# Layer 1's chunk recurrence with its small products grouped by array shape in a round, its value products one round ahead in a bank of their own, and part of its outputs on the other half of the partitions

## The chip, the cores and the metric

The kernel runs on one core of a Trainium2 chip, as one program with one launch. The metric is the device time in microseconds (us). The kernel before takes 2222.28 us (median of 3 runs, 2222.04 to 2224.26).

## The reference, cut to what matters

A trunk of two layers is run on a prompt of 1024 tokens (16 learned tokens ahead of it) and on a sample batch of 8 x 8 tokens. Layer 0 is a gated delta net, layer 1 an RWKV-7 mixer with 16 heads of 64. The change lies in the recurrence of layer 1:

```python
def step(S, inp):                       # one token; S is 64 x 64 for each head
    r_t, k_t, v_t, d_t, kk_t, b_t = inp
    S = (S * d_t[:, :, None, :]
         + jnp.einsum('bhvk,bhk->bhv', S, -kk_t)[..., None] * b_t[:, :, None, :]
         + v_t[..., None] * k_t[:, :, None, :])
    return S, jnp.einsum('bhvk,bhk->bhv', S, r_t)
S, y = lax.scan(step, S0, ...)
y = (y - mean) * lax.rsqrt(var + GN_EPS) * lnx_w + lnx_b      # group norm of each head
y = y + jnp.sum(r_h * k_h * r_k, -1, keepdims=True) * v_h     # bonus term
y = y.reshape(B, T, D) * jax.nn.silu(z)
return y @ w_o, ...                                           # dense output projection
```

## The kernel before

Layer 0 fills the program to about 1110 us; projections and the inverses of layer 1's chunk systems follow. The last part, from about 1800 to 2221 us, is the **wave**: layer 1's recurrence, with its output projection and part of the sample batch's state work laid between.

The tokens are cut in 3 segments of 6 chunks of 64 tokens, and the 16 heads in 8 pairs. One pair of one segment is an **item** `P`, 24 in all. The wave runs 52 **rounds**, `tau` 0 to 51; item n does its chunk steps `ci` 0 to 5 in rounds 2n to 2n+5. So three items are under way in each of 44 rounds (4 to 47), two in four rounds and one in four. Each engine runs its instructions in the order in which the code writes them. The order is written by hand: `put(tau, phase, f, prio)` books a piece of side work, `emit(tau, phase)` writes what is booked, and `fill` writes jobs of the output projection. A tile of that projection (`zo` or `do`) takes 12 matmuls with 384 columns, in two halves of 6, one in phase 2 and one in phase 3; DVE then adds it to the residual (`x<-x,zo`, line 2025).

A round does for each item, with 64 x 64 products that TensorE runs for the two heads `h` of the pair on two parts of its array:

- `step_solve`: state `rS` times `AR`, both for the system's right-hand side (`x` = 0) and for the output (`x` = 1), in the array shape 64 rows by 64 columns ("64*64" in the profile);
- `step_scores`: `UV` times `G`, the value part of the right-hand side ("128*64"), then ACT scales it into `X`;
- phase 1: side work, here the products `fG<-AR,BK` of a later item ("64*128"), every half item in one round, which DVE masks into `G` (line 1773);
- `step_inner`: `X` times the inverse `rTT` (128*64), then ACT copies the result into the U half of `UV` (line 115); `step_old` makes the decayed old state `pre`;
- phase 2: a dense half, and transposes of keys or values (`fBT`, `fVT`, 128*128);
- `step_state`: `UV` times `BT` for the new state and `UV` times `G` for the output (128*64); DVE writes `rS` (line 1906), ACT copies `y` (line 1907);
- phase 3: the other dense half, the bonus product `fbonus` with its DVE read `rbv` (line 1756), and at an item's end the transpose of `y` (`fyT`, 64*64) with its DVE read `t` (line 1937).

[...] In the wave, every item has one of the 3 banks `r` (tiles `rA`) for all its products of a round; 2 banks `f` take turns for `fG`, `fbonus`, `fBT`, `fVT` and `fyT`; one bank `z` and two banks `d` take the projection's tiles, and in the rounds up to 22 and from 30 to 38 the jobs for a segment's first four pairs use the one bank `z` alone. A reader of a bank and a writer of the same bank are kept apart by semaphores, whichever columns they touch.

A matmul on 32-bit floats is two instructions in the profile, so 4 products of an item are 8 instructions; the dense matmuls are one instruction each.

## Time and profile before

| | |
|---|---|
| median of 3 runs | 2222.28 us |
| profiled execution, its span | 2227.4 us, 5.1 us above the median (no other time of that execution is given) |
| the wave's share of the span | some 420 us, 52 rounds |
| PE busy over the span | 2142.1 us, 96% |
| DVE, ACT, POOL busy over the span | 1411.3, 1265.0, 1237.8 us |
| PE's share of the chain that ended last | 68% |
| DMA over the span | 129 GB/s from and to HBM |

The page counts an engine as busy while an instruction of it is under way, so a busy PE can still be a PE that waits for its own pipeline when the array's shape changes. A row of the timeline joins instructions of one kind that follow on each other: its start, the time until the last has ended, the group, and the number of instructions. The distance from one row's start to the next row's is what a group takes from the round. The ends of matmuls are modelled, and overlap the next group.

### The profile page before, as it was taken

The page shows a single profiled execution, that of the slowest core. Times are in us where ns is not written, and L with a number is a line of the kernel's source. Part 1 is how long each engine was busy: PE and PEld are TensorE (multiplying, and loading weights), DVE is VectorE, ACT ScalarE, POOL GpSimd, SP SyncE. Part 2 cuts the span into 40 slices and gives each one's busy share as a digit, 9 for nine tenths or more (in the row PEclk, how much of TensorE's full clock was granted, in tenths as well). Part 3 has the DMA queues.
Part 4 walks back from the last instruction along what each step waited for, and adds up shares of the span by engine and source line. Part 5 has one row for each costly group of instructions (what it writes and reads, how often), then busy time and mean ns, then how long its engine had stood idle before and what let it go on. Part 6 is the DMA issues. An engine that isn't in the chain of part 4 may idle for free.

```text
span 2227.4 us, 55333 instructions
## 1 busy us (share of the span) xinstructions
PE 2142.1 (96%) x20382; PEld 1977.4 (89%) x20382; DVE 1411.3 (63%) x3638; ACT 1265.0 (57%) x3651; POOL 1237.8 (56%) x1890
## 2 busy tenths in 40 slices
PE   8989999999999999989999999999999999999997
PEld 7879989899999989978999999998988977888886
DVE  7858575766757585975435762667546347667764
ACT  6526565556655565645433464756546466667663
POOL 3418678585858585525241442227768646666663
PEclk9999999999999999999999999999999999999997
DMA  4324242424243333435254235587885566656532
GB/s 120 84 59 133 66 123 73 114 80 115 79 115 96 101 107 76 132 78 171 91 151 105 69 102 172 180 256 199 229 242 147 160 187 166 171 150 177 160 115 88
DMA packets 495400, 291.61 MB, mean 131 GB/s; under 512 B 222345, under 2 KB 480506, under 8 KB 495130
## 3 DMA queue, kind: packets, MB, share of 16 engines
q1 hardware_dynamic: 495130, 288.08, 46.1%
q8 instruction: 161, 2.64, 0.5%
q14 instruction: 109, 0.89, 0.1%
HBM read 195.66 MB, written 92.30 MB: 129 GB/s over the span
## 4 chain that ended last, share of the span: by engine, by line
PE 68%; DVE 13%; POOL 6%; DMA 5%; ACT 4%; issue 3%; SPq 1%; DVEq 0%; POOLq 0%; ACTq 0%
PE d L129 14%; PE dz L129 7%; PE dv L129 7%; PE rA L133 6%; PE rA L129 5%; PE zo L129 3%; PE do L129 3%; PE dk L129 3%; DVE cvy L634 2%; POOL invT L692 2%; PE fG L129 2%; POOL invtmp L690 2%; PE dq L129 2%; DMA wraw<-in_gdn_w_out 1%; DVE invT L692 1%
## 5 line engine op out<-in xcount | busy, mean ns | idle before, releaser
L143 POOL TENSOR_TENSOR wlo<-wraw,whi 128x512 fp32r<-128x512 f32 x190 | 251.4, 1324 | 229.5 <-ACT whi L139 207.2
L692 POOL TENSOR_TENSOR invT<-invT,invtmp 72x31 f32<-72x31 f32 (+36 forms) x341 | 213.4, 626 | 26.7
L634 DVE SCALAR_TENSOR_TENSOR cvy<-raw,cw,cvy 128x408 f32<-128x408 f32 (+2 forms) x288 | 203.4, 706 | 29.7 <-ACT cvy L115 25.7
L690 POOL TENSOR_TENSOR invtmp<-invA,invT 72x31 f32<-72x31 f32 (+36 forms) x341 | 202.6, 594 | 20.4 <-POOL invT L678 0.8
L129 PE MATMUL d<-xc,whi 128*128 128x384 f32 (+1 forms) x640 | 180.8, 344 | 1.0 <-ACT whi L139 0.8
L139 ACT CAST whi<-wraw 128x512 fp32r<-128x512 f32 x238 | 145.7, 614 | 27.6 <-DMA wraw<-in_rwkv_w_rkvz 13.9
L129 PE MATMUL dv<-xc,whi 128*128 128x384 f32 (+1 forms) x480 | 154.5, 343 | 0.0
L129 PE MATMUL dz<-xc,whi 128*128 128x384 f32 (+1 forms) x480 | 153.0, 342 | 0.0
L115 ACT ACTIVATE w<-rA,nbp 128x128 f32<-128x128 f32 x144 | 45.2, 364 | 152.3 <-PE rA L129 149.9
L129 PEld LDWEIGHTS d<-xc,whi 128*128 128x128 f32 x640 | 118.6, 192 | 3.5 <-ACT whi L139 1.1
L129 PE MATMUL d<-xc,wlo 128*128 128x384 f32 (+1 forms) x320 | 105.5, 339 | 1.9 <-DVE wlo L143 1.9
L160 POOL TENSOR_TENSOR ors<-ovar,cvals 128x6 f32<-128x6 f32 x24 | 34.1, 1422 | 124.6 <-DVE ovar L1122 124.6
L129 PE MATMUL dz<-xa,whi 128*128 128x384 f32 (+1 forms) x288 | 102.6, 356 | 0.5 <-DVE zg L906 0.5
L129 PE MATMUL dv<-xa,whi 128*128 128x384 f32 (+1 forms) x288 | 102.5, 356 | 0.0
L129 PE MATMUL d<-xa,whi 128*128 128x384 f32 (+1 forms) x336 | 100.1, 341 | 1.3 <-ACT whi L139 0.8
L1930 POOL TENSOR_SCALAR y<-y,mv,grs 128x64 f32<-128x64 f32 x132 | 81.7, 640 | 33.1 <-DVE grs L164 27.8
L129 PEld LDWEIGHTS dv<-xc,whi 128*128 128x128 f32 x480 | 89.3, 188 | 3.5 <-issue 3.0
L959 POOL TENSOR_SCALAR Sb<-Sb,eglb 128x128 f32<-128x128 f32 x128 | 88.8, 706 | 5.9 <-DVE usc L752 2.2
L129 PEld LDWEIGHTS dz<-xc,whi 128*128 128x128 f32 x480 | 90.4, 191 | 0.7 <-issue 0.2
L129 PE MATMUL d<-xh,whi 128*128 128x384 f32 (+1 forms) x256 | 82.3, 334 | 0.0
L129 PE MATMUL d<-xl,whi 128*128 128x384 f32 (+1 forms) x256 | 82.3, 335 | 0.0
L129 PE MATMUL d<-xh,wlo 128*128 128x384 f32 (+1 forms) x256 | 82.1, 334 | 0.0
(544 smaller groups left out, 7232.1 us busy)
## 6 DMA issues: line engine op xcount, KB each, us to landing
wraw<-in_gdn_w_in SPq DMA_DIRECT2D x96, 256.0 KB
wraw<-in_rwkv_w_rkvz SPq DMA_DIRECT2D x74, 256.0 KB
Sb<-in_state_gdn SPq DMA_DIRECT2D x64, 256.0 KB
wraw<-in_rwkv_w_o SPq DMA_DIRECT2D x48, 256.0 KB
E<-drow SPq DMA_DIRECT2D x24, 384.0 KB
attn<-drow SPq DMA_DIRECT2D x24, 384.0 KB
wraw<-in_gdn_w_out SPq DMA_DIRECT2D x36, 256.0 KB
out_s_gdn<-Sb SPq DMA_DIRECT2D x32, 256.0 KB
```

Source lines behind the costliest of these rows:

```text
L115: return self.nc.scalar.activation(out, in_, func, bias=bias, scale=scale, **kw)
L129: self.nc.tensor.matmul(out, lhsT, rhs, start=start, stop=stop)
L133: self.nc.tensor.matmul(out, lhsT, rhs, start=start, stop=True, skip_group_check=True)
L139: nc.scalar.copy(hi, x)
L143: e.tensor_tensor(lo, x, hi.bitcast(F32), op=ALU.subtract)
L160: self.nc.gpsimd.tensor_tensor(y, x, half.broadcast_to(sh), op=ALU.pow)
L634: nc.vector.scalar_tensor_tensor(ys[s][:, 0:wd(s)], raws[s][:, k:k + wd(s)], cw[k], ys[s][:, 0:wd(s)], op0=ALU.mult, op1=ALU.add)
L690: v.tensor_tensor(tmp, A[:, j, j + 1:32].unsqueeze(2).broadcast_to([nb, n, m]), Tv[:, j, 0:m].unsqueeze(1).broadcast_to([nb, n, m]), op=AL ...
L692: v.tensor_tensor(Tv[:, j + 1:32, 0:m], Tv[:, j + 1:32, 0:m], tmp, op=ALU.subtract)
L959: nc.gpsimd.tensor_scalar(Sb[g][:, u], Sb[g][:, u], self.eglb[:, hv, 4 * g + u:4 * g + u + 1], None, op0=ALU.mult)
L1930: nc.gpsimd.tensor_scalar(y[:, q], y[:, q], mv[:, q, 0:1], P.rs[:, q:q + 1], op0=ALU.subtract, op1=ALU.mult)
```

## The change

The change touches only the wave.

- `step_scores` is gone. Its products become `step_values`, which runs for the items of the next round, right after `step_inner`, and writes to a bank `x` of its own (tiles `xX`). `step_solve` adds the state's part there, and `X` is read from it.
- With one bank for `x`, there are 2 banks `r` for three items: items 0 and 2 of a round share one (`P.bank = u % 2`), on different columns.
- The output part of `step_solve` (`x` = 1) goes to the other half of the array's columns and of the partitions (`hs[h ^ x]`). The products `fG` are cut in two and have the shape 64*64.
- `step_state` follows `step_values` directly; the dense half, the transposes and `step_old` that stood between inner and state come behind it.
- `fyT` writes the other half of the partitions and moves to phase 0 of round T+8, just ahead of `step_solve`; the add behind it moves to phase 1.
- The projection's jobs start half a round later, so that a tile's second half now stands in phase 2 and the next tile's first half in phase 3 of the same round. Two pieces of sample work move by a phase, and the urgent marks on `X` and `rS` go.

Counted in the order of the instructions, the changes of array shape on PE in the wave go from 421 to 169 (by the shape changed to: small shapes from 243 to 112, fG's 64*128 from 46 to 0, dense 128*128 with 384 columns from 95 to 48, transposes from 37 to 9).

The first place is PE between inner and state in a round of three items. `X`, `rTT` and `UV` are what is named above; the numbers are tiles. Before:

```order
L133 MATMUL rA_27066<-X_27067,rTT_4030_23640 64x64
L129 MATMUL do_27133<-yh_26107,whi_26840 128x384
L129 MATMUL do_27133<-yl_26108,whi_26840 128x384
L129 MATMUL do_27133<-yh_26107,wlo_26841 128x384
L129 MATMUL do_27133<-yh_26412,whi_26840 128x384
L129 MATMUL do_27133<-yl_26413,whi_26840 128x384
L129 MATMUL do_27133<-yh_26412,wlo_26841 128x384
L126 MATMUL fBT_27141<-ident_63,BK_26707 128x128 [waits DVE_49]
L126 MATMUL fBT_27141<-ident_63,BK_26707 128x128 x2
L133 MATMUL rA_27054<-UV_4025_23635,BT_26266 64x64 [waits Activation_49]
L133 MATMUL rA_27054<-UV_4025_23635,BT_26266 64x64
L133 MATMUL rA_27054<-UV_4025_23635,G_26075 64x64 x2
```

After:

```order
L133 MATMUL rA_27214<-X_27226,rTT_4030_23640 64x64 [waits Activation_49]
L133 MATMUL rA_27214<-X_27226,rTT_4030_23640 64x64
L133 MATMUL xX_27277<-UV_4026_23636,G_26502 64x64 [waits PE_49]
L133 MATMUL xX_27277<-UV_4026_23636,G_26502 64x64
L133 MATMUL xX_27277<-UV_4027_23637,G_26803 64x64 x2
L133 MATMUL xX_27277<-UV_4024_23634,G_27102 64x64 x2
L133 MATMUL rA_27214<-UV_4025_23635,BT_26401 64x64 [waits Activation_49]
L133 MATMUL rA_27214<-UV_4025_23635,BT_26401 64x64
L133 MATMUL rA_27214<-UV_4025_23635,G_26185 64x64 x2
L133 MATMUL rA_27215<-UV_4026_23636,BT_26713 64x64 x2
L133 MATMUL rA_27215<-UV_4026_23636,G_26502 64x64 x2
L133 MATMUL rA_27214<-UV_4027_23637,BT_27013 64x64 [waits Activation_49]
```

Six dense matmuls and three transposes stood between inner and state, and the waits are for each item's own copy. Now six value products stand there, and items 0 and 2 write the same tile: item 2's inner product waits for ACT's UV copy of item 0, item 0's state product for the UV copy of item 2, and item 2's state product for ACT's copy of item 0's `y`.

The second place is ACT in the same stretch. Before:

```order
L115 ACTIVATE UV_4025_23635<-rA_27054 64x128 [waits PE_49]
L115 ACTIVATE UV_4026_23636<-rA_27060 64x128 [waits PE_49]
L115 ACTIVATE UV_4027_23637<-rA_27066 64x128 [waits PE_49]
L115 ACTIVATE pre_27118<-rS_3947_23048,DC_25917 128x64 [waits Activation_49]
L115 ACTIVATE pre_27120<-rS_3948_23049,DC_26220 128x64 [waits Activation_49]
L115 ACTIVATE pre_27122<-rS_3949_23050,DC_26520 128x64 [waits Activation_49]
L139 CAST whi_27127<-wraw_26844 128x512 [waits DMAHW7_49]
L1782 COPY BT_27140<-fBT_27141 128x384 [waits PE_49]
L1907 COPY y_26356<-rA_27054 128x64 [waits DVE_49]
```

After:

```order
L115 ACTIVATE UV_4025_23635<-rA_27214 64x128 [waits PE_49]
L115 ACTIVATE UV_4026_23636<-rA_27215 64x128 [waits PE_49]
L115 ACTIVATE UV_4027_23637<-rA_27214 64x128 [waits PE_49]
L1923 COPY y_26485<-rA_27214 128x64 [waits DVE_49]
L1923 COPY y_26786<-rA_27215 128x64 [waits DVE_49]
L1923 COPY y_27085<-rA_27214 128x64 [waits DVE_49]
L1783 COPY BT_27312<-fBT_27313 128x384 [waits PE_49]
L115 ACTIVATE pre_27318<-rS_3948_23049,DC_26343 128x64 [waits Activation_49]
```

The three `pre` and the work that stood between the UV copies and the `y` copies moved behind the `y` copies; a `y` copy still waits for DVE, which updates `rS` from the same bank first.

The third place is PE at the seam of two rounds, in a round that ends an item's `y`. Before:

```order
L129 MATMUL fyT_27172<-ident_63,y_26051 64x64 x12
L126 MATMUL fBT_27188<-ident_63,BK_26707 128x128 x3
L133 MATMUL rA_27207<-rS_3948_23049,AR_26069 64x64 x4
L133 MATMUL rA_27213<-rS_3949_23050,AR_26374 64x64 x4
L133 MATMUL rA_27220<-rS_3950_23051,AR_26663 64x64 x4
L133 MATMUL rA_27207<-UV_4026_23636,G_26380 64x64 x2
L133 MATMUL rA_27213<-UV_4027_23637,G_26669 64x64 x2
L133 MATMUL rA_27220<-UV_4024_23634,G_26956 64x64 x2
L129 MATMUL fG_27244<-AR_26950,BK_26994 128x128
L129 MATMUL fG_27245<-AR_26950,BK_26994 128x128
```

After:

```order
L126 MATMUL fBT_27338<-ident_63,BK_26867 128x128 x3
L129 MATMUL fyT_27357<-ident_63,y_26168 64x64 x12
L133 MATMUL xX_27277<-rS_3948_23049,AR_26179 64x64 x2
L133 MATMUL rA_27372<-rS_3948_23049,AR_26179 64x64 x2
L133 MATMUL xX_27277<-rS_3949_23050,AR_26496 64x64 x2
L133 MATMUL rA_27373<-rS_3949_23050,AR_26496 64x64 x2
L133 MATMUL xX_27277<-rS_3950_23051,AR_26797 64x64 x2
L133 MATMUL rA_27372<-rS_3950_23051,AR_26797 64x64 x2
L129 MATMUL fG_27402<-AR_27096,BK_27166 64x128
L129 MATMUL fG_27403<-AR_27096,BK_27166 64x128
```

The transposes of `y` stay ahead of solve with the key transposes now in front of them; solve alternates between two tiles `xX` and `rA`, the value products between solve and `fG` are gone, and each `fG` product is half as wide in its weights. A bank `f` that `fyT` wrote is what the second `fG` tile takes over.

The diff, cut to its core:

```diff
             gp = [self.ps("f", 2, "G") for h in (0, 1)]
             for u in range(3):
-                for h in (0, 1):
-                    q = slice(64 * h, 64 * h + 64)
-                    self.mm(gp[h][:, 128 * u:128 * u + 128], flat(BK[q, c + u]), flat(AR[q, c + u]))
+                for x in (0, 1):
+                    for h in (0, 1):
+                        q, o = self.HS[h], self.HS[x]
+                        self.mm(gp[h][o, 128 * u:128 * u + 128], BK[q, c + u, x], flat(AR[q, c + u]))
             for h in (0, 1):
...
-            put(T - 1, 2, go, 5)
+            put(T - 1, 1, go, 5)
...
-            put(T + 2, 2, go2, 4)
+            put(T + 2, 1.5, go2, 4)
...
-            at = [(T + 6, 0, 2), (T + 6, 3, 4), (T + 7, 3, 2), (T + 8, 2, 0)]
+            at = [(T + 6, 0, 2), (T + 6, 2, 1.8), (T + 8, 0, 3), (T + 8, 1, 2.2), (T + 8, 2, 0)]
...
-    def step_solve(self, P, ci):
-        nc, t, ap = self.nc, self.t, self.ap
-        c = 6 * P.s + ci
-        if ci == 0:
-            P.y = t(ap, [128, 6, 64], "y", 5)
-        AR, S = P.AR, self.S[P.p]
-        pA = P.pA = self.ps("r", 3, "A")
-        X = P.X = t(ap, [128, 64], "X", 4)
-        hs = [slice(0, 64), slice(64, 128)]
-        if c != 1:
+    HS = (slice(0, 64), slice(64, 128))
+    def step_values(self, items):
+        p = self.ps("x", 1, "X") if items else None
+        for u, (P, ci) in enumerate(items):
+            P.pX = p[:, 64 * u:64 * u + 64]
+            for h in (0, 1):
+                self.mmx(P.pX[self.HS[h]], P.G[:, ci, h, 0:64], P.UV[:, ci, h, :], u == 0)
+    def first(self, P, part):
+        k = P.bank, part.start
+        new = k not in self.begun
+        self.begun.add(k)
+        return new
+    def step_solve(self, items):
+        t, ap, hs = self.t, self.ap, self.HS
+        self.begun = set()
+        banks = [self.ps("r", 2, "A") for _ in items[0:2]]
+        for u, (P, ci) in enumerate(items):
+            if ci == 0:
+                P.y = t(ap, [128, 6, 64], "y", 5)
+            P.bank, b = u % 2, 256 * (u // 2)
+            v = banks[u % 2]
+            P.pU, P.pY, P.pS = v[:, b:b + 128], v[:, b + 128:b + 192], v[:, b + 192:b + 256]
+            P.X = t(ap, [128, 64], "X", 4)
+            c = 6 * P.s + ci
+            S = self.S[P.p]
             for x in (0, 1):
                 for h in (0, 1):
-                    q = hs[h]
-                    a, b = (AR[q, ci, x], S[q]) if c else (P.q0[q, x].rearrange("p b r -> p (b r)"), self.ident[q, q])
-                    self.mmx(pA[q, 256 * x:256 * x + 64], a, b, x == 0)
-    def step_scores(self, P, ci):
-        nc, t, ap = self.nc, self.t, self.ap
-        c = 6 * P.s + ci
-        pA, X, G, UV, S = P.pA, P.X, P.G, P.UV, self.S[P.p]
-        hs = [slice(0, 64), slice(64, 128)]
-        for h in (0, 1):
-            self.mmx(pA[hs[h], 0:64], G[:, ci, h, 0:64], UV[:, ci, h, :], c == 1)
-        rk = self.rk2[:, 6 * P.n + ci:6 * P.n + ci + 1]
-        with self.tc.high_priority():
-            self.act(X, pA[:, 0:64], AF.Identity, scale=rk)
+                    if c == 1:
+                        continue
+                    q, o = hs[h], hs[h ^ x]
+                    l, r = (P.AR[q, ci, x], S[q]) if c else (P.q0[q, x].rearrange("p b r -> p (b r)"), self.ident[q, q])
+                    if x:
+                        self.mmx(P.pY[o], l, r, self.first(P, o))
+                    else:
+                        self.mmx(P.pX[o], l, r)
+        for P, ci in items:
+            rk = self.rk2[:, 6 * P.n + ci:6 * P.n + ci + 1]
+            self.act(P.X, P.pX, AF.Identity, scale=rk)
     def step_inner(self, items):
         for h, (P, ci) in [(h, x) for g in (items[0:2], items[2:]) for h in (0, 1) for x in g]:
-            self.mmx(P.pA[P.us, 128 + 64 * h:192 + 64 * h], P.TT[:, h, ci], P.X)
+            self.mmx(P.pU[P.us, 64 * h:64 * h + 64], P.TT[:, h, ci], P.X, self.first(P, P.us))
             if h:
-                self.act(P.UV[P.us, ci].rearrange("p h k -> p (h k)"), P.pA[P.us, 128:256], AF.Identity, scale=-1.0)
+                self.act(P.UV[P.us, ci].rearrange("p h k -> p (h k)"), P.pU[P.us], AF.Identity, scale=-1.0)
...
     def step_state(self, P, ci):
-        nc = self.nc
+        nc, hs = self.nc, self.HS
         c = 6 * P.s + ci
-        pA, G, BT, UV, S, DC = P.pA, P.G, P.BT, P.UV, self.S[P.p], P.DC
-        hs = [slice(0, 64), slice(64, 128)]
+        G, BT, UV, S, DC = P.G, P.BT, P.UV, self.S[P.p], P.DC
         if c > 0:
             for h in (0, 1):
-                self.mmx(pA[hs[h], 384:448], BT[:, ci, hs[h]], UV[:, ci, h, :])
+                self.mmx(P.pS[hs[h]], BT[:, ci, hs[h]], UV[:, ci, h, :], self.first(P, hs[h]))
         for h in (0, 1):
-            self.mmx(pA[hs[h], 256:320], G[:, ci, h, 64:128], UV[:, ci, h, :])
-        if c > 0:
-            with self.tc.high_priority():
-                if c == 1:
-                    nc.vector.tensor_scalar(S, pA[:, 384:448], DC[:, ci:ci + 1], None, op0=ALU.mult)
-                else:
-                    nc.vector.scalar_tensor_tensor(S, pA[:, 384:448], DC[:, ci:ci + 1], P.pre, op0=ALU.mult, op1=ALU.add)
-        nc.scalar.copy(P.y[:, ci], pA[:, 256:320])
+            self.mmx(P.pY[hs[1 - h]], G[:, ci, h, 64:128], UV[:, ci, h, :], self.first(P, hs[1 - h]))
+        if c == 1:
+            nc.vector.tensor_scalar(S, P.pS, DC[:, ci:ci + 1], None, op0=ALU.mult)
+        elif c > 0:
+            nc.vector.scalar_tensor_tensor(S, P.pS, DC[:, ci:ci + 1], P.pre, op0=ALU.mult, op1=ALU.add)
+        nc.scalar.copy(P.y[:, ci], P.pY)
...
             for h in (0, 64):
-                self.mm(yp[h:h + 64, 64 * q:64 * q + 64], y[h:h + 64, a + q], self.ident[h:h + 64, h:h + 64])
+                o = 64 - h
+                self.mm(yp[o:o + 64, 64 * q:64 * q + 64], y[h:h + 64, a + q], self.ident[h:h + 64, h:h + 64])
         t1 = t(self.fp, [128, 384], "t1", 1)
         nc.vector.scalar_tensor_tensor(t1[:, 0:n], yp[:, 0:n], self.lnw[:, p:p + 1], P.bv[:, x:x + n], op0=ALU.mult, op1=ALU.add)
+        yield
...
-            tag = [("d", 2), ("r", 3), ("d", 2)][q] if s == 2 else ("d", 2)
+            tag = [("d", 2), ("r", 2), ("d", 2)][q] if s == 2 else ("d", 2)
...
-        jobs += [(lambda s=s, a=a: out(s, a, a + 4, *((Z, DD) if a else (Z,))), 16, 14 + 16 * s + 2 * a, 22 + 16 * s + 2 * a) for s in (0, 1) for a in (0, 4)]
+        jobs += [(lambda s=s, a=a: out(s, a, a + 4, *((Z, DD) if a else (Z,))), 16, 14.5 + 16 * s + 2 * a, 22.5 + 16 * s + 2 * a) for s in (0, 1) for a in (0, 4)]
...
+        at = lambda tau: [(P[n], tau - 2 * n) for n in range(max(0, (tau - 4) // 2), min(24, tau // 2 + 1)) if 0 <= tau - 2 * n < 6]
         emit(-4, 3)
         for tau in range(-2, 52):
-            items = [(P[n], tau - 2 * n) for n in range(max(0, (tau - 4) // 2), min(24, tau // 2 + 1)) if 0 <= tau - 2 * n < 6]
-            each = lambda f: [f(*x) for x in items]
+            items, following = (at(u) for u in (tau, tau + 1))
             if tau < 0:
                 fill(tau + 0.3)
             emit(tau, 0)
-            each(self.step_solve)
-            each(self.step_scores)
+            self.step_solve(items)
             emit(tau, 1)
             self.step_inner(items)
-            each(self.step_old)
+            self.step_values(following)
+            for x in items:
+                self.step_state(*x)
+            emit(tau, 1.5)
             put(tau, 2, lambda: fill(tau + 0.5), 2.5)
             emit(tau, 2)
-            each(self.step_state)
+            for P_, ci in following:
+                self.step_old(P_, ci)
             put(tau, 3, lambda: fill(tau + 1), 1)
...
```

8 lines of the change are left out of this document (5 added, 3 removed).

## The prediction

> **What bounds the kernel now.** I read the page's totals first, then the wave by windows, then the order of PE's groups in two rounds with the ACT and DVE rows beside them.
>
> ```profile
> span 2227.4 us, 55333 instructions
> PE 2142.1 (96%) x20382; PEld 1977.4 (89%) x20382; DVE 1411.3 (63%) x3638; ACT 1265.0 (57%) x3651; POOL 1237.8 (56%) x1890
> 1919.60:2166.40 246.80, 246.09 (x3736) 213.99 (x3734) 171.16 (x579) 168.72 (x571) 159.04 (x197) 1.00 0.54 153
> ```
>
> The last row is a stretch of the wave: its bounds, its length, then busy time and count of PE, PEld, DVE, ACT and POOL, the granted clock, the DMA share and GB/s. PE is busy for 246.09 of 246.80 us at full clock; the others have a third free. The wave is bound by PE, so what counts is how long each group takes PE from its start to the next start. One round, on PE:
>
> ```profile
> 1964.86 0.91 PE L133 MATMUL rA<-rS,AR 64*64 64x64 f32 x24
> 1965.70 0.57 PE L133 MATMUL rA<-UV,G 128*64 128x64 f32 x12
> 1966.20 0.94 PE L129 MATMUL fG<-AR,BK 64*128 64x128 f32 x12
> 1967.07 0.68 PE L133 MATMUL rA<-X,rTT 128*64 128x64 f32 x12
> 1967.67 0.44 PE L129 MATMUL zo<-yh,whi 128*128 128x384 f32 x1
> ...
> 1968.65 0.34 PE L129 MATMUL zo<-yh,wlo 128*128 128x384 f32 x1
> 1968.83 0.49 PE L126 MATMUL fVT<-ident,fldv 128*128 128x128 f32 x3
> 1969.25 0.34 PE L133 MATMUL rA<-UV,BT 128*64 128x64 f32 x4
> ...
> 1969.65 0.29 PE L133 MATMUL rA<-UV,G 128*64 128x64 f32 x4
> 1969.77 0.29 PE L133 MATMUL rA<-UV,BT 128*64 128x64 f32 x4
> 1969.88 0.29 PE L133 MATMUL rA<-UV,G 128*64 128x64 f32 x4
> ...
> 1971.08 0.34 PE L129 MATMUL zo<-yh,wlo 128*128 128x384 f32 x1
> 1971.26 0.34 PE L129 MATMUL fbonus<-prh,bones 128*128 128x384 f32 x1
> 1971.43 0.34 PE L129 MATMUL fbonus<-prl,bones 128*128 128x384 f32 x1
> 1971.70 0.92 PE L133 MATMUL rA<-rS,AR 64*64 64x64 f32 x24
> ```
>
> In a steady stretch (1969.65, 1969.77, 1969.88) four small instructions take 0.117 us, on two parts of the array at once: 0.0585 for one instruction on its part. BT and G alternate there with no gap, so tiles and operands may change freely; the array's shape may not. Solve's 24 instructions should take 0.70 and take 0.84; scores' 12 should take 0.35 and take 0.50. Six dense ones take 1.16 (1967.67 to 1968.83), not 6 x 0.173 = 1.04 (spacing of the `fbonus` rows), and leaving that shape costs 0.27 - 0.173 = 0.10 (1971.43 to 1971.70). A change of shape thus costs about 0.145 towards a small one. To dense it is 0.10 to drain and 0.11 to load, 0.205. `fG` takes 0.87 for six pairs at about 0.11 (twice the columns), so 0.20. Transposes, between the two, I put at 0.152.
>
> **Change: what it saves.**
>
> Shape changes. Before: 243 x 0.145 + 46 x 0.20 + 95 x 0.205 + 37 x 0.152 = 69.5 us. After: 112 x 0.145 + 48 x 0.205 + 9 x 0.152 = 27.4. Saved on PE's path: **42.1**.
>
> Solve on four parts. It uses rows by h, columns by h and x, so all four 64x64 parts work at once, where two did. That four run together is seen once before, in layer 0:
>
> ```profile
> 105.31 0.64 PE L129 MATMUL usr<-Sb,kqm 128*32 128x128 f32 x16
> 105.89 0.45 PE L129 MATMUL dv<-xc,whi 128*128 128x384 f32 x1
> ```
>
> Sixteen instructions of 128 columns, each on a quarter of the columns, take 0.58, which is four times 0.11 and one change; two at a time they would take 0.88. For solve: 1088 instructions x 0.0585 x (1/2 - 1/4) = **15.9**, 0.35 in a round of three. `fG` has twice the instructions on twice the parts: nothing. The value products are the same number, only earlier: nothing. At the bounds, these two terms are 0 (parts that share rows don't overlap) and 15.9.
>
> **Change: what it makes wait.** `fVT`, `fBT` and a dense half, 1.58 us by the rows above (1967.67 to 1969.25), lay between inner and state and hid ACT's UV copies. Now 0.35 of value products lie there, and three items have two banks. The prices:
>
> ```profile
> L115 ACT ACTIVATE UV<-rA x144: 255/272/276, 1801.9 to 2195.6; 64x128 f32<-64x128 f32 x144
> L1907 ACT COPY y<-rA x144: 204/213/243, 1804.9 to 2201.1; 128x64 f32<-128x64 f32 x144
> L1906 DVE SCALAR_TENSOR_TENSOR rS<-rA,DC,pre x128: 268/284/288, 1815.7 to 2200.8; 128x64 f32<-128x64 f32 x128
> L133 PE MATMUL rA<-X,rTT x576: 222/222/367, 1801.4 to 2195.0; 128*64 128x64 f32 x192
> ```
>
> The middle figure is the median in ns. A round in which nothing dense stands between inner and state occurs once before, near the end, and shows the chain bare:
>
> ```profile
> 2145.49 0.85 PE L133 MATMUL rA<-X,rTT 128*64 128x64 f32 x12 [0.18 <-ACT X L115]
> 2146.07 0.86 ACT L115 ACTIVATE UV<-rA 64x128 f32<-64x128 f32 x3 [0.23 <-PE rA L133]
> 2146.40 0.34 PE L133 MATMUL rA<-UV,BT 128*64 128x64 f32 x4
> ```
>
> From inner's start 0.91 us go by until the first state product. By the medians, with 0.05 for a hop between engines (2146.07 + 0.27 + 0.05 = 2146.39, against 2146.40 seen), a round of three items then runs like this, counted from inner's start:
>
> - Item 0's last inner product starts at 0.17, ends at 0.39; UV0 runs 0.44 to 0.71. Item 2's inner product, in the same bank, starts at 0.76, not 0.23: **0.53**.
> - It issues for 0.23, ends at 1.16; UV2 runs 1.20 to 1.47. The value products end issuing at 1.34, so item 0's state product waits until 1.53: **0.19**.
> - Item 0's state ends 0.40 after its start; DVE begins `rS` 0.12 later (in the rows below 1976.25 + 0.29 to 1976.66) and takes 0.28, the `y` copy 0.25 with its hop. Items 0 and 1 issue 0.47. Item 2's state waits **0.64**.
>
> Three restarts, each with a weight load that nothing covers, add 0.13 (an estimate: about a third of the 0.145 that a shape change costs). Together 1.49 us in each of 44 rounds: **65.4**. Queued behind PE's waits is the whole round, since PE runs in order; ACT's next work, `pre` and the key copy, has slack. The bounds are 0 (if all of it were covered) and 75 (if each hop took 0.10).
>
> The banks `f` and `z` are next. Rows of one seam:
>
> ```profile
> 1971.46 0.55 DVE L2025 TENSOR_TENSOR x<-x,zo 128x384 f32<-128x384 f32 x1 [0.89 <-PE zo L129]
> 1971.93 0.55 DVE L1756 TENSOR_TENSOR rbv<-fldv,fbonus 128x384 f32<-128x384 f32 x1
> 1974.02 1.02 DVE L1773 TENSOR_TENSOR G<-fG,gm 128x384 f32<-128x384 f32 x2 [1.06 <-PE fG L129]
> 1976.25 0.29 PE L133 MATMUL rA<-UV,G 128*64 128x64 f32 x4
> 1976.66 0.74 DVE L1906 SCALAR_TENSOR_TENSOR rS<-rA,DC,pre 128x64 f32<-128x64 f32 x3
> 1978.17 0.92 PE L129 MATMUL fyT<-ident,y 64*64 64x64 f32 x24
> 1979.22 0.61 DVE L1937 SCALAR_TENSOR_TENSOR t<-fyT,lnw,rbv 128x384 f32<-128x384 f32 x1
> 1979.49 0.27 PE L133 MATMUL rA<-rS,AR 64*64 64x64 f32 x2
> ```
>
> - `fG`'s second tile needs the bank that `fbonus` left. From the last `fbonus` (1971.43) to the end of `rbv` 1.05 pass, 1.10 with the hop. Before, solve and scores covered it (1.61 to `fG`). Now the drain (0.27) and the halved solve (0.50 with its change) end after 0.78: 0.32 in 23 odd rounds, **7.3**.
> - In even rounds `fyT` stands just ahead of solve, and `fG` takes its bank. From `fyT`'s start to the end of `t` are 1.66, 1.71 with the hop; fyT's 24 instructions and solve issue for 0.84 + 0.35 = 1.19: 0.52 in 19 rounds, **9.9**. `t` then holds DVE; with the two `G` masks (1.02 at 1974.02) and group-norm work behind it, `rS` comes about 0.35 late there, **6.6** (an estimate: a third of the 1.02, since most of it passes while PE waits and issues).
> - In the 16 rounds whose projection uses bank `z` alone, the next tile's first half follows the last one's second half with three transposes between: 0.17 and the 0.33 that `fVT`'s 0.42 takes without the drain behind it, 0.50. The residual add begins 0.38 after the last product's start (1971.08 to 1971.46) and takes 0.55: 0.98 with the hop, so 0.48 x 16 = **7.7**. Before, the other way round, solve to inner lay between.
>
> One of these waits occurs before, a few times, and shows that PE does stand still for it:
>
> ```profile
> 1832.28 0.93 PE L129 MATMUL fG<-AR,BK 64*128 64x128 f32 x10 [0.27 <-DVE rbv L1756]
> ```
>
> **The rest.** The moved phases of sample work issue the same DMAs on SP's queue a phase earlier or later; their data are needed rounds later, and neither queue waits: 0, at most 1 us either way. The urgent marks only ordered instructions, and the order is what I used. The `finish` tag with two banks instead of three serves one tile in the last 6 us: 0 to 0.5. Waits of before that go (some 3 us in rounds like that at 2145) balance those new in the eight rounds of one or two items.
>
> **Sum.** -42.1 - 15.9 + 65.4 + 7.3 + 9.9 + 6.6 + 7.7 = +38.9 us on the profiled 2227.4, so 2266 for a profiled span; on the median 2222.3 it is **2261 us**. As a round pair: solve to the solve after next takes 14.63 us before (1964.86 to 1979.49); 58.0/22 = 2.64 less and 96.9/22 = 4.40 more make 16.4. The likeliest case's own range is 2245 to 2278, from a chain of 1.1 to 1.9 us for a round.
>
> **Rivals.**
>
> *Faster: the chain is covered.* Savings less the other waits are 58.0 - 31.5 = 26.5, so it turns at 26.5 / 44 = 0.60 us of bank waits a round. It would take one of item 2's three waits alone (0.64 at the state) with the others hidden, say by ACT and DVE starting on products well before the modelled ends of the rows. Gone entirely it gives 2196; at a third of my price (0.3 us a round) 2209. Against: at 2145.49 the first state product came 0.91 after inner's start though item 0's X was there. For: the ends are modelled, and a part of the 0.91 is the wait for the later items' X.
>
> *Slower still: the clock.* Where PE idled, the trace shows the clock fall:
>
> ```profile
> 1909.78 1.64 PE L129 MATMUL fG<-AR,BK 64*128 64x128 f32 x10 [1.75 <-DVE rbv L1756]
> 1905.00:1910.00 5.00, 3.25 (x40) 2.67 (x42) 2.06 (x6) 2.09 (x8) 1.61 (x2) 0.96 0.83 240
> 1910.00:1913.00 3.00, 3.00 (x24) 2.66 (x25) 2.87 (x9) 0.88 (x4) 2.70 (x4) 0.50 0.01 3
> ```
>
> After 1.75 us of idle PE the next 3 us ran at 0.50. An even round of mine idles for some 2.4 of 8.8 us in pieces of under 0.7. If those pieces add up, a stretch of 3.4 us at half speed costs 1.7 us in 22 rounds, +37: 2298. Against: no piece is nearly 1.75 long.
> [...]
>
> *Four parts don't overlap.* Solve's saving goes (hidden in `fG`'s wait in most rounds), and `fG` takes 0.67 longer in 46 rounds, +31: 2292. Against: the `usr` row.
>
> *Even.* Bank waits near 1.0 us a round in place of 1.49, and half of the other waits, give 2222 - 58 + 44 + 16 = 2224.
>
> *Grouping saves nothing.* The waits alone without the 42: 2303. Against: `fVT` follows dense work of its own shape with no gap (1968.65 by the spacing of 0.173 to 1968.83).
>
> **How the numbers follow.** Likeliest (2245 to 2278 and its edges) 0.63; faster 0.14; clock 0.12; four parts 0.05; even 0.04; no gain by grouping 0.02. Runs agree to about 0.2% (4.4 us), my bound for "same". Faster 0.14, same 0.04 and slower 0.82. The range takes in the even case, the upper half of the faster one and most of the clock's: 2209 to 2300 leaves out about 0.07 below and 0.09 above.
>
> **What would show it.** PE's share in the wave falls from near 100% to about 85%, with some 75 us of idle time. The waits before `rA<-X,rTT` and `rA<-UV,BT` would name ACT, at 0.5 and 0.6 us, and those before `fG` DVE, 0.3 to 0.5. Solve would take 0.35 to 0.40 in a round of three, and `fG` 0.66 beside its wait. The granted clock should stay 1.00. It would be wrong if item 2's inner product starts within 0.3 us of item 0's, if state follows the value products without a wait, or if the clock falls below 0.9 in the steady part.

## The result, and the profile after

The changed kernel takes 2285.54 us (median of 4 runs, 2274.95 to 2290.45), the kernel before 2223.27. The ratio is 1.0273, with a 95% interval of 1.025 to 1.0296; on another chip, later, it was 1.0307 (1.0276 to 1.0339). The forecast was 2261 us, in a range of 2209 to 2300: slower, as said, and inside the range, but 24 us above the forecast value.

The page's totals after:

```profile
span 2286.3 us, 56349 instructions
PE 2129.9 (93%) x20958; PEld 1959.2 (86%) x20958; DVE 1417.3 (62%) x3638; ACT 1266.3 (55%) x3651; POOL 1232.1 (54%) x1890
```

PE does more instructions and is busy for less time, in a longer span. The wave, from the first inner product to the last, in one row each of before and after (length, busy time and count of PE, PEld, DVE, ACT, POOL, then granted clock, DMA share, GB/s):

```profile
1801.40:2195.00 393.60, 383.02 (x5655) 326.65 (x5653) 264.62 (x873) 258.50 (x852) 237.90 (x296) 0.98 0.56 155
```

```profile
1790.50:2250.50 460.00, 383.71 (x6195) 320.53 (x6193) 268.67 (x870) 260.27 (x852) 232.39 (x294) 0.95 0.47 132
```

The wave grew by 66.4 us. PE is idle for 76.3 us of it, where it was idle for 10.6. (The stretch ahead of the wave, which the change doesn't touch, was 11 us shorter in this execution; in the second profile of the same kernel it was 2 us shorter. 41 us of that stretch were at half clock, against 68 in the profile before, with the same program.) What PE waited for in the wave, in us, times, and the longest:

```profile
PE rA L133 <- ACT y L1923: 28.0, 44, 1.4
PE rA L133 <- ACT UV L115: 21.1, 45, 2.3
PE fG L129 <- DVE t L1954: 8.2, 17, 1.3
PE zo L129 <- DVE x L2043: 4.1, 13, 0.3
```

44 waits for a `y` copy and 45 for a UV copy: one of each in a round of three items. Before, no row of this list named ACT's `y` or UV copies ahead of a product of the recurrence. One odd round after, with ACT's and DVE's rows:

```profile
2021.49 0.27 PE L133 MATMUL xX<-rS,AR 64*64 64x64 f32 x2
2021.89 1.20 PE L129 MATMUL fG<-AR,BK 64*64 64x128 f32 x24
2022.40 0.72 ACT L115 ACTIVATE X<-xX,rk 128x64 f32<-128x64 f32 x3
2023.01 0.53 ACT L115 ACTIVATE fDp<-fldcs 128x384 f32<-128x384 f32 x1
2023.02 0.45 PE L133 MATMUL rA<-X,rTT 128*64 128x64 f32 x8
2023.42 0.53 ACT L115 ACTIVATE fiD<-fldcs 128x384 f32<-128x384 f32 x1
2023.84 0.56 ACT L115 ACTIVATE UV<-rA 64x128 f32<-64x128 f32 x2
2024.15 0.39 PE L133 MATMUL rA<-X,rTT 128*64 128x64 f32 x3 [0.68 <-ACT UV L115]
2024.43 0.52 PE L133 MATMUL xX<-UV,G 128*64 128x64 f32 x11
2024.64 0.27 ACT L115 ACTIVATE UV<-rA 64x128 f32<-64x128 f32 x1 [0.24 <-PE rA L133]
2024.96 0.34 PE L133 MATMUL rA<-UV,BT 128*64 128x64 f32 x4
2025.36 0.29 PE L133 MATMUL rA<-UV,G 128*64 128x64 f32 x4
2025.55 0.47 DVE L1922 SCALAR_TENSOR_TENSOR rS<-rA,DC,pre 128x64 f32<-128x64 f32 x2 [0.39 <-PE rA L133]
2025.86 0.40 ACT L1923 COPY y<-rA 128x64 f32<-128x64 f32 x2 [0.96 <-DVE rS L1922]
2026.13 0.34 PE L133 MATMUL rA<-UV,BT 128*64 128x64 f32 x4 [0.48 <-ACT y L1923]
```

Solve on four parts takes 0.40 us (2021.49 to 2021.89), where it took 0.84. Item 2's inner product starts at 2024.15, 1.13 after inner's start: it waits for UV0, which itself stands on ACT behind two exponentials for a later item (`fDp`, `fiD`, 2023.01 to 2023.84). Its state product starts at 2026.13, 0.77 after the start of item 1's last group (2025.36), behind `rS` and then `y` of item 0. An even round has the wait of `fG` for the read of `fyT`'s bank:

```profile
2012.85 0.74 PE L129 MATMUL fyT<-ident,y 64*64 64x64 f32 x18
2013.82 0.62 DVE L1954 SCALAR_TENSOR_TENSOR t<-fyT,lnw,rbv 128x384 f32<-128x384 f32 x1 [1.14 <-PE fyT L129]
2014.49 0.88 PE L129 MATMUL fG<-AR,BK 64*64 64x128 f32 x22 [0.33 <-DVE t L1954]
2015.30 0.45 PE L133 MATMUL rA<-X,rTT 128*64 128x64 f32 x8
2016.10 0.39 PE L133 MATMUL rA<-X,rTT 128*64 128x64 f32 x3 [0.35 <-ACT UV L115]
```

For all kernels below I split the wave in one way, from the start of every matmul in each trace. "Steady" is each instruction at its spacing in a steady stretch (0.02925 us for a small one with two parts at work, half of it for solve and `fG` with four, and so on). "Changes" is what the distances at changes of array shape, and behind them to the second dense product, have above that. "Waits" is the rest; it holds also the slower start of each group, 0.107 us from its first products to the next in place of 0.0585, behind a change as behind a wait. "Half clock adds" is half of the time at half clock, an estimate (in the changed kernel's trace the dense product `d` starts every 0.320 us at half clock and every 0.174 at full), and stands apart. In us:

| kernel | steady | changes | waits | sum | half clock adds |
|---|---|---|---|---|---|
| before | 291.2 | 56.7 (409) | 36.1 | 384.0 | 9.6 |
| changed | 275.3 | 24.6 (161) | 136.5 | 436.4 | 23.6 |
| changed, second profile | 275.4 | 24.8 (161) | 139.4 | 439.5 | 15.7 |
| 1 products ahead of readers | 275.4 | 25.0 (161) | 99.1 | 399.5 | 8.1 |
| 2 as 1, with cover | 275.4 | 41.2 (263) | 72.4 | 389.0 | 7.7 |
| 3 y transposes back | 275.3 | 29.4 (203) | 132.0 | 436.7 | 14.5 |
| 4 own banks | 291.1 | 35.3 (250) | 68.5 | 395.0 | 6.8 |
| 5 as 2, y transposes and jobs back | 275.4 | 44.7 (300) | 58.5 | 378.5 | 14.8 |
| 6 as 5, solve on two parts | 291.2 | 44.6 (300) | 41.4 | 377.2 | 11.6 |
| 7 as 5, fG whole | 275.4 | 50.7 (351) | 52.1 | 378.2 | 11.9 |
| 8 as 5, earlier loads | 275.4 | 44.6 (300) | 56.2 | 376.3 | 15.1 |
| 10 as changed, state ahead only | 275.4 | 25.0 (161) | 109.4 | 409.7 | 9.0 |
| 11 as changed, inner ahead only | 275.4 | 24.8 (161) | 138.0 | 438.2 | 17.1 |

(In brackets, the number of changes of shape.)

### The profile page after: what moved, and what is told of

Read it like the earlier page. It is cut to its first block, busy times and chain, and to the rows that moved or that the text cites. A ratio compares the mean times of both kernels' runs of the same rounds, so it can differ in the third digit from the quotient of the medians.

```text
span 2286.3 us, 56349 instructions
## 1 busy us (share of the span) xinstructions
PE 2129.9 (93%) x20958; PEld 1959.2 (86%) x20958; DVE 1417.3 (62%) x3638; ACT 1266.3 (55%) x3651; POOL 1232.1 (54%) x1890
## 3 DMA queue, kind: packets, MB, share of 16 engines
q1 hardware_dynamic: 495130, 288.08, 44.7%
## 4 chain that ended last, share of the span: by engine, by line
PE 58%; DVE 17%; ACT 7%; POOL 7%; DMA 5%; issue 4%; SPq 1%; DVEq 0%; POOLq 0%; ACTq 0%
PE d L129 11%; PE dz L129 7%; PE dv L129 7%; PE rA L129 6%; PE do L129 3%; PE zo L129 3%; POOL invtmp L690 3%; POOL invT L692 3%; DVE cvy L634 2%; PE rA L133 2%; PE dk L129 2%; PE dq L129 2%; PE fG L129 1%; DMA wraw<-in_gdn_w_out 1%; DVE invtmp L690 1%
## 5 line engine op out<-in xcount | busy, mean ns | idle before, releaser
L634 DVE SCALAR_TENSOR_TENSOR cvy<-raw,cw,cvy 128x408 f32<-128x408 f32 (+2 forms) x288 | 201.2, 699 | 31.4 <-ACT cvy L115 27.4
L129 PE MATMUL dk<-xc,whi 128*128 128x384 f32 (+1 forms) x240 | 80.1, 352 | 0.0
## 6 DMA issues: line engine op xcount, KB each, us to landing
E<-drow SPq DMA_DIRECT2D x24, 384.0 KB
attn<-drow SPq DMA_DIRECT2D x24, 384.0 KB
```

The costliest lines, as they stand in the source:

```text
L129: self.nc.tensor.matmul(out, lhsT, rhs, start=start, stop=stop)
L634: nc.vector.scalar_tensor_tensor(ys[s][:, 0:wd(s)], raws[s][:, k:k + wd(s)], cw[k], ys[s][:, 0:wd(s)], op0=ALU.mult, op1=ALU.add)
```

## The experiments

The theory: two banks for three items make PE wait three times a round for a reader of the other item, and these waits are larger than what the grouping saves. Rivals: the dense cover between inner and state is what is missing, whoever shares a bank; or the loss lies in `fG`'s waits and the clock.

**1. All products ahead of their readers.** Inner's six products are written before the three copies, state's twelve before the `rS` updates and `y` copies.

```diff
         for h, (P, ci) in [...]:
             self.mmx(P.pU[...], P.TT[:, h, ci], P.X, self.first(P, P.us))
-            if h:
-                self.act(P.UV[...], P.pU[P.us], ...)
+        for P, ci in items[1:2] + items[0:1] + items[2:]:
+            self.act(P.UV[...], P.pU[P.us], ...)
...
-            for x in items:
-                self.step_state(*x)            # products, rS update, y copy
+            for x in items[1:2] + items[0:1] + items[2:]:
+                self.step_state(*x)            # products
+            for x in items[1:2] + items[0:1] + items[2:]:
+                self.step_read(*x)             # rS update, y copy
```

> The changed kernel, with inner's six products of a round all ahead of the three UV copies, and state's twelve all ahead of the rS updates and y copies (item 1 first, then 0 and 2). Same products, same two shared banks, same shapes; only item 2 no longer has to wait for a reader of item 0. Theory (the shared bank makes PE wait for UV0 and y0, some 1.5 us in a round of three): one wait of 0.3 to 0.5 us before the first state product of items 0 and 2 is left, so about 1.1 x 44 = 48 us go, and some half-clock time with them: 2235 us, 2220 to 2245. Rival (what is missing is the cover of the dense half, whoever shares a bank): PE waits as long, now in one place ahead of state; 2270 to 2290. Rival (fG's waits and the clock are the loss): 2275 or more.

Measured: 2236.74 us, ratio 1.008 (1.0064 to 1.0096). Waits fall by 37 us, with not one product, bank or shape changed, and no wait for `y` is left among the listed ones:

```profile
PE zo L129 <- DVE x L2052: 12.6, 16, 1.4
PE fG L129 <- DVE t L1963: 9.0, 17, 1.3
PE rA L133 <- ACT UV L115: 7.2, 12, 2.6
```

The order of writes and reads in the shared bank costs that much, and neither missing cover nor `fG`'s waits and the clock explain it: those rivals said 2270 or more. (The order of the items changed with it; cover with the change's own order was not run.) But the wait for bank `z` grew from 4.1 to 12.6 idle us; why was not followed up.

**2. The same with the dense half as cover.** `emit(tau, 1.5)` and phase 2 move up between `step_values` and `step_state`.

```diff
             self.step_values(following)
+            emit(tau, 1.5)
+            put(tau, 2, lambda: fill(tau + 0.5), 2.5)
+            emit(tau, 2)
             for x in ...:
                 self.step_state(*x)
...
-            emit(tau, 1.5)
-            put(tau, 2, lambda: fill(tau + 0.5), 2.5)
-            emit(tau, 2)
```

> As the first, and the dense half with phase 2's transposes stands again between the value products and state. Theory: the whole chain from inner to state is hidden, the waits for UV and y go to under 0.1 us a round; two more changes of shape a round (0.35 us) come back: 2285 - 65 + 15 - 10 for the clock is about 2225, range 2205 to 2235; against the first kernel -10 to +10. Rival (cover is what counts): as low as that here, with the first kernel left at 2270 or more. Rival (fG's waits and the clock): 2255 or more.

Measured: 2223.04 us, ratio 1.0023 (1.0004 to 1.0042). Waits fall by another 27 us and changes come back with 16. Cover and order are both worth something; the whole chain is gone with both.

**3. The transposes of y back in the round before.**

```diff
-  (T + 6, 2, 1.8), (T + 8, 0, 3), (T + 8, 1, 2.2)
+  (T + 6, 2, 1.8), (T + 7, 3, 2), (T + 8, 1, 2.2)
```

> The changed kernel with only the transposes of y (fyT) moved back from just ahead of solve to phase 3 of the round before. Theory: fG's wait for the read of fyT's bank (0.52 us in 19 even rounds in the prediction, 8.2 us in all in the trace) goes, and rS comes earlier in even rounds: -8 to -16 us, 2270 to 2278. Rival: the two changes of shape that come back (0.3 us in 22 rounds) eat it: within 5 us of 2285.

Measured: 2282.26 us, ratio 1.0284 (1.0262 to 1.0305), the same as the change within the intervals. Waits fall by 4.5, changes rise by 4.8: the rival held. Whatever this move costs in waits it earns in shapes.

**4. Own banks.** The value products go back behind solve in their own round, bank `x` goes, and each item has its bank again. The outputs return to the half that they had.

```diff
-        banks = [self.ps("r", 2, "A") for _ in items[0:2]]
...
+            P.bank = u
+            v = self.ps("r", 3, "A")
+            P.pX, P.pU, P.pY, P.pS = v[:, 0:64], v[:, 128:256], v[:, 256:320], v[:, 384:448]
...
-            self.step_values(following)        # now inside step_solve, for items, into P.pX
```

> The changed kernel with its value products back behind solve in their own round, no bank x, three banks r with one for each item, and the outputs on the half they had. State still follows inner with nothing between, fG stays in 64x64 parts, the dense halves stay where the change put them. Theory: item 2 waits for no copy of item 0; left is the wait for each item's own UV copy, about 0.35 to 0.5 us a round, against 1.5; against it stand solve on two parts (+16, some hidden in fG's wait) and about one more change of shape in the rounds with fG: 2285 - 46 + 12 - 8 for the clock = 2243, range 2225 to 2258. Rival (cover is what counts): without even the value products between inner and state it gets slower still, 2295 or more.

Measured: 2232.48 us, ratio 1.0057 (1.0039 to 1.0075). Waits are 68 us lower than in the changed kernel, although nothing at all stands between inner and state. That rules the rival of the cover out once more. This run takes back the bank `x`, the value products' lead of a round and the outputs' half together; that the banks are what cost rests on experiment 1 and on the waits by name.

**The changed kernel again**, for a second profile.

> The changed kernel as it is, for a second profile beside the others. The first shows 41 us of the recurrence at half clock, which cost 24 us of time at full clock's rate, against 24 and 10 in the kernel before. Theory (PE's many short waits bring the clock down now and then): again 30 us or more at half clock between the first and the last inner product, and a time of 2275 to 2290. Rival (it was chance in one execution): 24 us or less at half clock, as before, and a time 10 us below.

Measured: 2293.41 us, ratio 1.0307, above the 2290 that the theory allowed; 31.4 us of the wave at half clock, which cost 15.7. (The 41 and 24 us of the expectation count the stretches that begin in the wave; 47.2 and 19.2 us lie in it.) That is the 30 us of the theory, but the kernels 5 and 8, with less than half of the waits, spent 29.7 and 30.2 us at half clock too. In kernel 5 each dip follows a single wait of 1.2 to 5.0 us, the longest ahead of the dip at 1898.9; so the sum of the waits alone doesn't give the time at half clock. What the traces show ahead of a fall stands below, with the prediction's clock term. In this second profile the rounds from 1880 to 2220 us ran at full clock throughout, PE idle for 57 of 340 us:

```profile
1880.00:2220.00 340.00, 283.00 (x4855) 234.55 (x4852) 206.04 (x672) 199.62 (x664) 180.89 (x231) 1.00 0.47 134
```

**5. Cover, y transposes and jobs back.** As 2, with 3's edit, and the projection's jobs from 14 again.

```diff
-  16, 14.5 + 16 * s + 2 * a, 22.5 + 16 * s + 2 * a)
+  16, 14 + 16 * s + 2 * a, 22 + 16 * s + 2 * a)
```

> The second kernel (products ahead of their readers, dense half between value products and state), with the transposes of y back in phase 3 of the round before, and the projection's jobs starting at 14 and not 14.5, so that a tile's two halves stand in one round again. Theory (what is left in the second kernel are waits for the banks f and z: 11 us before fG and 8 us before the dense half behind state): fG's wait goes against changes of shape of about the same size (-3 us as in the third kernel), the z wait goes (-7): 2213 us, 2205 to 2220, the first below the kernel before by a measurable amount. Rival (the waits move elsewhere, to X or to rS): 2220 to 2226, no better than the second kernel.

Measured: 2216.31 us, ratio 0.9971 (0.9956 to 0.9987): faster than the kernel before by 0.3%. The waits for `z` are gone, and those of `fG` for `t`; what is left before `fG` is for `rbv`.

**6. Solve on two parts.** As 5, with the output products on the half of the right-hand side.

```diff
-                    q, o = hs[h], hs[h ^ x]
+                    q, o = hs[h], hs[h]
...
-            self.mmx(P.pY[hs[1 - h]], ...)
+            self.mmx(P.pY[hs[h]], ...)
```

> The kernel with products ahead, cover, y transposes back and jobs at 14, but solve's output products on the same half of the columns as its right-hand side, so that solve runs on two parts of the array and not on four; state's output and the y transposes follow onto that half. Everything else alike. Theory (four parts save 0.35 us a round where nothing waits behind solve): +12 to +16 us on the kernel with four parts. Rival (the saving is lost in waits of fG or inner for X that come behind solve): within 5 us.

Measured: 2218.52 us, ratio 0.9972 (0.9955 to 0.999), the same as 5, as the rival said. Steady work rises by the 15.8 us that four parts save, and waits fall by 17.1. The seam of an odd round shows why; first kernel 5, then kernel 6:

```profile
2032.69 0.34 PE L129 MATMUL fbonus<-prl,bones 128*128 128x384 f32 x1
2033.42 0.55 DVE L1756 TENSOR_TENSOR rbv<-fldv,fbonus 128x384 f32<-128x384 f32 x1
2033.63 1.27 PE L129 MATMUL fG<-AR,BK 64*64 64x128 f32 x23
2034.83 0.39 PE L133 MATMUL rA<-X,rTT 128*64 128x64 f32 x5
```

```profile
2009.04 0.34 PE L129 MATMUL fbonus<-prl,bones 128*128 128x384 f32 x1
2009.54 0.55 DVE L1756 TENSOR_TENSOR rbv<-fldv,fbonus 128x384 f32<-128x384 f32 x1
2010.05 0.96 PE L129 MATMUL fG<-AR,BK 64*64 64x128 f32 x24
2010.94 0.50 PE L133 MATMUL rA<-X,rTT 128*64 128x64 f32 x9
```

In kernel 5 `fG`'s row starts 0.94 after `fbonus` (2032.69 to 2033.63) but its second bank is free only when `rbv` ends at 2033.97, so the group takes 1.20 until inner starts. In kernel 6 solve takes longer, `fG` starts later, just as `rbv` ends (2010.09), and takes 0.89. From `fbonus` to inner pass 2.14 and 1.90, the shorter time with the slower solve, since DVE came to `rbv` 0.23 earlier there. In these two rounds DVE sets the end of the seam, and a faster solve only waits longer for it.

**7. fG whole.** As 5, with `fG` in 64*128.

```diff
-                for x in (0, 1):
-                    for h in (0, 1):
-                        q, o = self.HS[h], self.HS[x]
-                        self.mm(gp[h][o, ...], BK[q, c + u, x], flat(AR[q, c + u]))
+                for h in (0, 1):
+                    self.mm(gp[h][:, ...], flat(BK[q, c + u]), flat(AR[q, c + u]))
```

> The same kernel with products ahead, cover, y transposes back and jobs at 14, but the fG products whole again (64*128, 12 instructions and not 24). Theory (a product costs the same either way, and only changes of shape count): one more change of shape in each of some 45 rounds, at 0.12 of drain and 0.05 of load: +5 to +8 us, unless a wait for X behind fG swallows it. Rival (the forecast's 0.20 for each change towards 64*128 holds): +9 or more. Rival (24 instructions on four parts are slower than 12 on two): a gain.

Measured: 2217.53 us, ratio 0.9977 (0.9959 to 0.9995). Changes cost 6.0 us more and waits 6.4 less: the expected price, and swallowed by the same seam.

**8 and 9. Earlier loads of the residual**, in kernel 5 and in the kernel before. The load of the final norm's weights moves behind them, and segment 1's go two rounds ahead.

```diff
-            nc.sync.dma_start(self.fw, ...final_norm_w...)      # in gates()
+        put(19, 3, norm_load, 9)
+        put(28, 3, lambda: residual(1), 9)                      # loads of x2[:, 0:3]
```

> The kernel with products ahead, cover, y transposes back and jobs at 14, with the residual's first loads earlier: the 512 KB load of the final norm's weights no longer stands ahead of segment 0's, and segment 1's go out two rounds before its first projection tile. In the fifth kernel's trace DVE waits 6.5 us for two of these loads, rbv stands behind that wait, and PE stands 5.0 and 1.45 us before fG. Theory (what is left of fG's wait is DVE held by a DMA): -5 to -8 us against the fifth kernel, 2209 us, 2203 to 2214. Rival (the load comes late for another reason, the queue's order or its buffers): within 3 us of it.

> The kernel before with the same earlier loads and nothing else. There DVE waits 4.7 us for the two loads, and PE 1.8 us at one place, with some 7 us at half clock behind it. Theory: -2 to -5 us, 2217 to 2220. Rival (PE has other work there and nothing is gained): 2221 to 2224. The difference to the first kernel of this call is then what the change's parts bring without their waits.

Measured: 2215.50 us, ratio 0.9962 (0.9942 to 0.9983), and 2220.55 us, ratio 0.9991 (0.997 to 1.0013). Neither differs from its base by what can be told. (Kernel 9 is not in the table: its wave takes 390.7 us, 4.9 of them for half clock; the 385.8 left stand against 384.0.) The second of the two DMA waits went, the first, the longer one, stayed in the eighth kernel and in the ninth:

```profile
DVE x L2052 <- DMA x<-x1T: 4.2, 1, 4.2
```

```profile
DVE x L2025 <- DMA x<-x1T: 3.7, 1, 3.7
```

So the load of the final norm's weights was not what held it. The traces show the loads issued only when DVE needs them: SP issues segment 0's at 1895.26 in kernel 5, where DVE stands idle from 1895.22, and at 1903.88 in kernel 8, where it stands from 1904.20. The edit took the norm's load away and left these in their place in SP's order.

**10 and 11. One half of experiment 1 each**: only state's products ahead, or only inner's.

> The changed kernel with only state's products ahead of the rS updates and y copies; inner and its UV copies as the change has them. Theory (the three bank waits are separate and measured in the trace at 29, 10 and 35 us): the 35 us before item 2's state product go, the other two stay: about 1.0155 times the kernel before, 2255 us, 2248 to 2264. Rival (one chain, and what is taken from one wait comes back in the next): 2275 or more.

> The changed kernel with only inner's products ahead of the UV copies; state as the change has it. Theory: the 29 us before item 2's inner product go; the UV copies start later, so the wait before the first state product grows from 0.21 to about 0.5 us, 13 us in all: net -16, 2272 us, 2263 to 2280. With the 35 of state that makes the first kernel's 50. Rival (one chain): 2285 or more.

Measured: 2249.74 us, ratio 1.0118 (1.0079 to 1.0158), and 2281.85 us, ratio 1.0252 (1.0216 to 1.0288). The waits of state alone first, then those of inner alone:

```profile
PE rA L133 <- ACT UV L115: 24.3, 47, 2.7
PE fG L129 <- DVE t L1960: 9.0, 17, 1.3
```

```profile
PE rA L133 <- ACT UV L115: 31.7, 47, 2.9
PE rA L133 <- ACT y L1923: 29.6, 44, 1.6
```

The wait for `y` is a wait of its own, as the theory said: without it 27 us of waits go, of the 34.9 before item 2's state product; the rest comes back in smaller waits, as those for `z`, from 4.1 to 7.0 idle us. Inner alone gains nothing that can be told, between the theory's 2280 and the rival's 2285. The two for UV copies are one chain: with inner ahead, the copies start after the last inner product and run one behind the other, and the wait ahead of the first state product grows from 0.21 us (47 times) to 0.71 (50 times), nearly all that was gained. The expectation had 0.5 us there; item 0's copy comes first, but item 0's state needs item 2's, the last. Both halves together give more (experiment 1) than the sum of each, probably since item 1's state, now first, stands in the wait for UV2; that was not tried by itself.

## Why the prediction was right, and where it was off

*What bounds it.* PE's time from start to start, as said; the share of busy PE in the wave fell to 83% (85% was named), with 76.3 us idle (75).

*Shape changes, -42.1.* The measured term is -32.1 (56.7 to 24.6), at 409 to 161 changes. The count was right (421 and 169, with the ends of the wave). The price was too high: 56.7 / 409 = 0.139 us on the average, the distance to the second dense product included, against 69.5 / 421 = 0.165. It had been read from whole groups (0.84 for 0.70), and such a group holds, beside the distance at the change itself (0.148 us from solve's last start to scores' first, before), the slower spacing of its first instructions, which it keeps when it is no longer preceded by another shape but by a wait (the 0.107 above, in place of 0.0585).

*Solve on four parts, -15.9.* The size was right: in solve's rows four instructions start every 0.0585 us where two did, and with that the steady work falls from 291.2 to 275.3. The rival that four parts don't overlap is out, by the 0.40 us above. But kernel 6 shows that where the bank waits are gone this saving is worth nothing, because `fG` waits at the seam.

*The bank chain, +65.4 and +6.6 for a late rS.* All three waits are there, in the places named. Worked out from the same starts, item 2's inner product waits 29.2 us in the wave, item 0's state 9.7, item 2's state 34.9, and the restarts behind them 3.6: 77.4 against 72.0. Item 2's inner was put too low, at 0.53: in odd rounds ACT's exponentials stand between `X` and UV (1.13 to its start), and the prediction gave ACT's other work slack without placing it on ACT's queue. The late `rS` is there too: item 2's state waits 0.70 in most odd rounds, 0.75 or 1.10 in the even ones. That 37 us go with the order, and 68 with the banks given back (experiments 1 and 4), is what shows this term.

*fG's and z's waits, +7.3, +9.9 and +7.7.* Measured 11.3 for `t` (20 times 0.565; 19 times 0.52 was said) and 6.3 for `z` (14 times 0.45; 16 times 0.48). The wait for `rbv` is there, but inside `fG`'s group, where it can't be parted from the group's own spacing.

*The clock, 0 in the sum.* Half clock added 23.6 and 15.7 us in the two profiles against 9.6 before: 6 to 14 us that the sum didn't have. The rival priced at +37, a dip in every even round, did not occur: from 1880 to 2220 us the second profile shows 1.00 and the first three dips of 3.4 us. But the first of these three came behind short idle pieces alone. In the traces every change of the clock lies a whole number of steps of 3.413 us behind the first one (to within 5 ns; 33 changes before, 39 in the changed kernel). The first of the three dips, with the step ahead of it:

```profile
2004.99:2008.40 3.41, 2.03 (x43) 1.63 (x41) 2.04 (x10) 1.81 (x7) 1.97 (x4) 1.00 0.07 19
2008.40:2011.81 3.41, 3.41 (x12) 3.31 (x13) 2.00 (x5) 0.82 (x3) 0.00 (x0) 0.50 0.37 115
```

PE was idle for 1.38 of 3.41 us, in two pieces: 0.88 for a UV copy and 0.48 for a `y` copy. Counted over the wave of all fourteen traces, in these steps (idle by the modelled ends), half clock followed all 34 full-clock steps with 1.8 us of idle PE or more, 26 of 118 with 1.0 to 1.8, and 1 of 1435 with less (in the first profiles of before and after alone 2 of 2, 8 of 16 and 0 of 211). In the second profile no step from 1880 to 2220 has more than 1.37. So the largest of its steady rounds' steps lie in the middle group; what separates the 26 from the other 92 is not shown.

*Sum.* -15.9 - 32.1 + 100.4 + 14.0 = +66.4 us for the wave of this profile, where -15.9 - 42.1 + 96.9 = +38.9 was said. The steps that were off are the price of a shape change (10 us), the clock (6 to 14) and ACT's queue (about 5), all to the same side. So the result lies above the likeliest case's own range of 2245 to 2278, and inside the stated one only because that took in most of the clock rival. The mechanism stands: waits for a shared bank outweigh two real savings.

The faster rival needed bank waits of under 0.60 us a round; they are 77.4 / 44 = 1.76. Its other half was right in kind: with the chain covered and its order changed (kernel 5), the new grouping is faster than the kernel before, by 0.3%. But the 2196 us named for it were too good, as kernel 5 is at 2216: the cover brings changes of shape back, and the seam keeps its waits.

## What to carry to other kernels

Before products are laid closer together, write down for each bank who reads it, and whether the next write there has to wait for that reader: here the order of writes and reads in a shared bank was worth more than the grouping of the shapes (37 us of waits for an order, 32 for 248 changes). When several items share a bank, issue all their products first and read them afterwards. And a saving on the busiest engine counts only up to the next thing that has to be released by another: solve became twice as fast (0.40 us, for 0.84 with its change of shape), and the time went into waiting for a read on DVE.

## What the runs showed of the hardware that had not been expected

Four 64x64 parts of the array ran four 32-bit streams at once: in solve four instructions started every 0.0585 us where two did, and its 24 took 0.40 us against 0.84 with its change of shape before. A change of shape cost 0.139 us on the average of 409, the distance to the second dense product included; the distance at the change itself was 0.09 to 0.15 above steady spacing for the common pairs of shapes (from start to start, before: 0.148 us from solve to scores, 0.202 from `fG` to inner, 0.268 from `fbonus` to solve). The clock stayed at 1.00 over 340 us in which PE idled for 17% of the time in pieces of up to 1.4 us, yet fell in the first profile, at 2008.40, behind pieces of 0.88 and 0.48 us in one step of 3.41 us.
